# Differential attention over cached keys: scores in pairs of sequences, values in three pieces

## The chip, the core and the metric

One kernel on one NeuronCore of a Trainium2 chip. The metric is the device time of one execution in microseconds (us). TensorE multiplies, VectorE (DVE), ScalarE (ACT) and GpSimd (POOL) do the rest, SyncE (SP) issues most of the transfers. Each engine works through its own list of instructions in order and waits where an operand, a buffer or a transfer isn't ready.

## The reference, cut to the part that matters

The kernel is one layer of a decoder for a prompt of 512 rows and eight sample sequences of 4 new rows each. The part at issue is the differential attention of the samples: each sequence scores its 4 new rows against 256 cached keys (two pages, found through a page table) and its own 4 new keys, in four heads of two 64-wide components; the two softmaxes are subtracted with a factor, and the result is multiplied with the cached and new values.

```
def diff_attend(q, k, v, mask, lam):
    s = jnp.einsum('bqhcd,bkhcd->bhcqk', q, k) * (DA_QK_DIM ** -0.5)
    s = jnp.where(mask[None, None, None], s, -jnp.inf)
    p = jax.nn.softmax(s, axis=-1)
    a = p[:, :, 0] - lam * p[:, :, 1]
    return jnp.einsum('bhqk,bkhd->bqhd', a, v)

def da_attend_sample(q, k, v, lam, past_k, past_v):
    kk = jnp.concatenate([past_k, k], axis=1)
    vv = jnp.concatenate([past_v, v], axis=1)
    return diff_attend(q, kk, vv, kpos[None, :] <= qpos[:, None], lam)
```

## The kernel before

The layer runs in stages: memory keys, mixer input projections, the mLSTM heads, the differential attention with the output projection behind it, cross-attention, and the gated MLP with its convolution. All is fp32 data; large products are made from split weights (a rounded part and a remainder, `split`, lines 144 to 147), so each weight slot passes over ScalarE (cast, L146) and VectorE (remainder, L147) after its transfer.

The differential attention runs two pipelines side by side. The prompt's pipeline (`prompt`, 16 units, one for each of four blocks of rows and four heads; unit i has block i // 4) makes for each unit two score tiles (`da_soft`: product L1211, causal mask L1212, maximum L1214, exponential L1215, combination of the two softmaxes L1217 to L1219), two steps later a turn of the probabilities (`da_turn`, `tpa`, L1227, copied by ScalarE at L1229), one step later the product with the values (`da_av`, `oda`, L1237), and after each block's last head the normed block (`da_post`, `dat`, L1081). The samples' pipeline has eight sequences: the gathers of two key pages (`dk_load`, through `gather`, L1069), their turn into a key tile (`dk_turn`, `tpk`, L1191, copied by ScalarE or VectorE at L1192), and the scores (`dk_scores`, `ssc`, L1197: four heads, each a 32-column instruction into its own 32 partitions, then mask L1199, maximum L1035, exponential L1036). Then follow the softmax of all sequences (`sample_softmax`) and the values (`dv_load`, `dv_out`, `ops`, L1279), again four heads of 32 columns each, for two pages of each sequence; the new keys' values come last (L1287). Both pipelines share five PSUM buffers (`mmp`) for `ssc`, `sda`, `tpa` and `oda`, and three (`at`) for the turns of keys and others.

The gathers of keys and values and the weights' transfers go through one pool of six staging buffers (`stage`, `wst`), in the order of the program: eight key tiles, eight value tiles, then the slots of `w_out`. A tile takes over the buffer of the one six places ahead, and SyncE's list holds these transfers in that order. The turned keys lie in the pool of weight slots (`wp`, four buffers); `W.nslots` limits how many weight slots are fetched ahead. `w_out` is added to the plan only after the samples' values (L1300), and its first product is `proj` (L407 to L409).

The order within each engine's list is set by a scheduler from the order of the program and from priorities; `burst(t)` puts what it holds right behind the instruction t.

Of the kernel before, what the change touches and what calls it, by code (L numbers as in the profile page):

```python
# [15 lines left out]
P = 128  # L16
DM = 1024
SEQ = 512
NB = 8
TS = 4  # L20
NS = NB * TS
ROWS = SEQ + NS
H = 4
# [54 lines left out]
def kernel(ctx: ExitStack, tc: tile.TileContext, I, O):  # L78
    nc = tc.nc
    MUL, ADD, SUB, MAX, MIN = ALU.mult, ALU.add, ALU.subtract, ALU.max, ALU.min  # L80
# [27 lines left out]
    def T2(shape, name, dt=F32):  # L108
        return t2p.tile(list(shape), dt, name=name, tag="T2")
# [4 lines left out]
    def at(name="at"):  # L114
        return psa.tile([P, 512], F32, name=name, tag="at")

    def mmp(name="mm"):
        return psm.tile([P, 512], F32, name=name, tag="mm")
# [8 lines left out]
    def v2(t, b):  # L127
        return t.rearrange("p (a b) -> p a b", b=b)

    mm = nc.tensor.matmul  # L130
    tr = nc.tensor.transpose
    VTT = nc.vector.tensor_tensor
# [22 lines left out]
    def con(n, p=P):  # L155
        o, w = CONST_COLS[n]
        return cpk[:p, o:o + w]
# [49 lines left out]
    W = Weights(NSLOT)  # L207
# [132 lines left out]
    @contextmanager  # L340
    def burst(ins):

        if ins is None:
            yield
        else:
            with tc.issue_after(ins), tc.high_priority():
                yield
# [252 lines left out]
    dvS, kNs = ta[:NS, 0, :], ta[:NS, 1, :]  # L600
# [53 lines left out]
    for c0, c1 in HALF:  # L654
        n = c1 - c0
        ps = mmp()
# [3 lines left out]
        t = T2([64, n], "gt")  # L660
# [38 lines left out]
        in1=v2(Mx[:, 0:SEQ - P], P)[:, :, P - 1:P].broadcast_to([H, 3, P]), op=ADD)  # L699
# [8 lines left out]
    ps = at("gtp")  # L708
# [3 lines left out]
    ps = at("gtp")  # L712
# [190 lines left out]
    ps = at("npt")  # L903
# [7 lines left out]
    for g in range(2):  # L911
        for h in range(0, H, 2):
            t = stage().rearrange("p (j b e) -> p j b e", j=2, b=4)
# [27 lines left out]
    ps = at("nT0")  # L941
# [10 lines left out]
    t = None  # L952
    for h in range(H):
        with burst(t):
            t = mm(pg[NS * h:NS * h + NS, P:2 * P + 1], lhsT=sm_t[:, h, :], rhs=vNs[:, h, :], start=True, stop=True).ins
    for h in range(H):
        with burst(t):
            t = mm(pg[NS * h:NS * h + NS, 4:12], lhsT=qT[:, h, SEQ:], rhs=nT[:, h, :], start=True, stop=True).ins
    for b in range(NB):
        for h in range(H):  # L960
            with burst(t):
                t = mm(pi[NS * h:NS * h + NS, 0:P], lhsT=qzm[:, 256 * h + b * NS:256 * h + (b + 1) * NS],
                       rhs=csts[b // 4, h][:, b % 4, :], start=(b == 0), stop=(b == NB - 1)).ins
# [12 lines left out]
    ps = at("nTt")  # L976
# [17 lines left out]
    r, ss = gq[:, 14:15], gq[:, 15:16]  # L994
# [39 lines left out]
    def sample_exp(sall, b, ps, nm, su):  # L1034
        VRED(out=nm[:, b:b + 1], in_=ps, axis=AX.X, op=MAX, negate=True)  # L1035
        ACT(out=sall[:, b, :], in_=ps, func=AF.Exp, bias=nm[:, b:b + 1], accum_out=su[:, b:b + 1])  # L1036
# [126 lines left out]
    qz = sm.tile([P, H, 2, 2, 16], F32, name="qz", tag="qz", bufs=1)  # L1163
# [8 lines left out]
    for b in range(4):  # L1172
        c = slice(b * P, b * P + P)
# [3 lines left out]
    kst, kts, pts, aTs, outs, rcs = {}, {}, {}, {}, {}, {}  # L1177
# [14 lines left out]
            (VCP if g else nc.scalar.copy)(out=kt[:, :, g * P:(g + 1) * P], in_=v2(ps, P))  # L1192

    def dk_scores(b):
        ps = mmp("ssc")[:, :260]
        for h in range(H):
            mm(ps[NS * h:NS * h + NS], lhsT=qz[:, h, b // 4].rearrange("p c r -> p (c r)"), rhs=kts[b][:, h, :],  # L1197
               start=True, stop=True)
        VTT(out=ps[:, 256:260], in0=ps[:, 256:260], in1=con("cm4"), op=ADD)  # L1199
        sample_exp(sall, b, ps, nm, su)  # L1200

    def da_soft(i):
        b, h = i // H, i % H
# [41 lines left out]
    cv = cst.tile([P, 1], F32, name="cv")  # L1245
    STT(out=cv, in0=con("cB"), scalar=nlam, in1=con("cA"), op0=MUL, op1=ADD)

    W.nslots = 2
    prompt = pipe(4 * H, da_soft, lambda i: None, da_turn, da_av, da_end)
    sall = S([P, NB, 260], F32, "das")  # L1250
    nm, su = small(NB, "snm"), small(NB, "ssu")
    for t, _ in enumerate(pipe(NB, dk_load, dk_turn, dk_scores)):
# [5 lines left out]
    aw, az = sample_softmax(sall, su, cv, con("selD"), "da")  # L1258
# [3 lines left out]
        in1=con("selB").unsqueeze(2).broadcast_to([P, NB, TS]), op=MUL)  # L1262
    nps = at("npn")
    tr(nps[:NS, :P], pz, ident)
    anew = sm.tile([NS, H, NB, TS], F32, name="anew", tag="anew", bufs=1)
    VCP(out=anew, in_=nps[:NS, :P].rearrange("p (b h t) -> p h b t", b=NB, h=H))

    ops = at("ops")
    vts = {}

    def dv_load(b):
        st = vts[b] = stage()
        for g in range(2):
            gather("cache_dv", b, g, st[:, 512 * g:512 * g + 512])

    def dv_out(b):
        for g in range(2):
            for h in range(H):
                mm(ops[NS * h:NS * h + NS, :P], lhsT=az[g][:, h, b * NS:(b + 1) * NS],  # L1279
                   rhs=vts[b][:, g * 512 + h * P:g * 512 + (h + 1) * P], start=(b == 0 and g == 0), stop=False)  # L1280

    for t, _ in enumerate(pipe(NB, dv_load, lambda b: None, dv_out)):
        if t % 2 == 0:
            next(prompt, None)
        F.run(2)
    for h in range(H):
        mm(ops[NS * h:NS * h + NS, :P], lhsT=anew[:, h].rearrange("p b t -> p (b t)"), rhs=dvS[:, h * P:(h + 1) * P],  # L1287
           start=False, stop=True)
    oS = T2([P, P], "daoS")
    nc.scalar.copy(out=oS, in_=ops[:, :P])  # L1290
    sq = T2([P, P], "dasq")
# [2 lines left out]
    ps = at("dat")  # L1294
# [107 lines left out]
    kst, kts, vts = {}, {}, {}  # L1402
# [46 lines left out]
    sall = S([P, NB, 256], F32, "cas")  # L1449
    nm, su = small(NB, "snm"), small(NB, "ssu")  # L1450
# [11 lines left out]
    for b in range(4):  # L1462
        t = mk_scores(b)
    with tc.issue_after(t):
        for j in range(8, 16):
            t = mk_turn(j)
# [7 lines left out]
    with tc.issue_after(t):  # L1474
        for b in range(4, NB):
            t = mk_scores(b)
# [3 lines left out]
    with tc.high_priority():  # L1480
        _, az = sample_softmax(sall, su, None, con("selX"), "ca")
# [15 lines left out]
    ps = at("ost")  # L1497
    for e in range(2):
        tr(ps[:, e * P:(e + 1) * P], oS[:, e * P:(e + 1) * P], ident)
    ps = ps[:, :256].rearrange("p (e h n) -> p h e n", e=2, n=NS)  # L1500
# [20 lines left out]
    for t0 in (0, 4):  # L1521
        ps = at("cvp")
# [5 lines left out]
    ps = at("cvp")  # L1528
# [145 lines left out]
    for gi, js in enumerate(groups):  # L1674
# [47 lines left out]
        if not last:  # L1722
            behind = []
            for n0 in (0, 512):
# [3 lines left out]
                ps = [mmp() for _ in range(4)]  # L1728
                for i in range(nk):
# [3 lines left out]
                    for b in range(4):  # L1733
                        t = one(b, ps[b], i, s)
# [5 lines left out]
            ps = {n0: at("sdn") for n0 in (0, 512)}  # L1740
# [57 lines left out]
        t = chunk(TORD[1], 0)  # L1798

        for n0 in (0, 512):  # L1800
            with burst(t.ins):
                t = chunk(TORD[0], n0)
# [77 lines left out]
```

## Time and profile before

| | us |
|---|---|
| median of 3 runs | 958.01 (953.81 to 958.31) |
| the profiled execution's own time | 956.79 |
| its span in the profile | 955.0 |
| TensorE busy in the span | 932.7 (98%) |
| VectorE busy | 599.2 (63%) |
| ScalarE busy | 388.8 (41%) |
| GpSimd busy | 197.5 (21%) |

The differential attention lies between 246 and 331 us of the span. A busy share is a mean over the stages; how near TensorE is to its limit in one stage is read from its busy time in that stretch, and who holds it up from the waits named beside its rows. Rows of the timeline give start, duration, engine, line, operation and operands; a duration of TensorE reaches into the next instruction, so costs are taken from start to start.

### The profile page before, as it was taken

What the parts mean: (1) busy time and instruction counts of PE and PEld (TensorE: products, weight loads), DVE (VectorE), ACT (ScalarE), POOL (GpSimd) and SP (SyncE); (2) the same over time, 40 slices, a digit from 0 to 9 for tenths busy, and PEclk for the clock granted to TensorE, in tenths of its full rate; (3) what the DMA queues carried; (4) which work ended last, traced back from release to release, by engine and by line L of the source; (5) the groups of instructions that cost most, each with busy time, mean ns of one, the idle gap of its engine ahead of it and who ended that gap; (6) DMA issues with size and microseconds to landing.
All of it is one profiled execution on the core that took longest, in us unless ns stands there. A gap on an engine that the chain in (4) does not pass through costs nothing. (4 is left out here: it accounts for less than half of the span.)

```text
span 955.0 us, 17088 instructions
## 1 busy us (share of the span) xinstructions
PE 932.7 (98%) x6619; PEld 810.6 (85%) x6619; DVE 599.2 (63%) x1129; ACT 388.8 (41%) x750; POOL 197.5 (21%) x383
## 2 busy tenths in 40 slices
PE   8999999999999999999999999999999999999995
PEld 5899777879866778998777799989988997999974
DVE  5745144565887448635654769727758676676867
ACT  5655133344676447624544523332212222222232
POOL 6610000024432217300000444001110110111114
PEclk9999999999999999999999999999999999999998
DMA  8950023334825429955953743063053302512023
GB/s 278 309 184 2 1 89 136 89 110 150 264 90 183 155 94 329 307 155 167 353 213 114 206 134 89 4 177 89 4 144 79 122 26 79 165 48 89 24 92 116
DMA packets 120674, 130.27 MB, mean 136 GB/s; under 512 B 8568, under 2 KB 86233, under 8 KB 120593
## 3 DMA queue, kind: packets, MB, share of 16 engines
q1 hardware_dynamic: 114408, 125.69, 41.9%
q10 hardware_dynamic: 6184, 3.48, 1.2%
q8 instruction: 52, 0.85, 0.4%
q14 instruction: 30, 0.24, 0.1%
HBM read 112.22 MB, written 16.93 MB: 135 GB/s over the span
## 5 line engine op out<-in xcount | busy, mean ns | idle before, releaser
L146 ACT CAST wslot<-wst 128x1024 fp32r<-128x1024 f32 x125 | 130.9, 1050 | 259.9 <-issue 74.7
L477 PE MATMUL mm<-fT,wslot 128*128 128x256 f32 x1872 | 235.9, 288 | 0.0
L477 PEld LDWEIGHTS mm<-fT,wslot 128*128 128x128 f32 x1872 | 234.4, 188 | 1.8 <-issue 0.8
L147 DVE TENSOR_TENSOR wslot<-wst,wslot 128x1024 fp32r<-128x1024 f32 x125 | 155.1, 1245 | 89.3 <-ACT wslot L146 88.8
L1691 PE MATMUL mm<-wslot,act 128*128 128x512 f32 (+1 forms) x180 | 70.2, 391 | 0.0
L1692 PE MATMUL mm<-wslot,act 128*128 128x512 f32 (+1 forms) x180 | 70.0, 392 | 0.0
L1690 PE MATMUL mm<-wslot,act 128*128 128x512 f32 (+1 forms) x180 | 69.3, 387 | 0.0
L1598 POOL COPY cvo<-u 128x2 f32<-128x2 f32 x43 | 11.0, 256 | 204.8 <-DVE u L1596 194.7
L407 PE MATMUL mm<-wslot,hT 128*128 128x512 f32 x128 | 52.2, 408 | 0.0
L409 PE MATMUL mm<-wslot,hT 128*128 128x512 f32 x128 | 51.5, 403 | 0.0
L408 PE MATMUL mm<-wslot,hT 128*128 128x512 f32 x128 | 51.3, 401 | 0.0
L477 PE MATMUL mm<-hT,wslot 128*128 128x256 f32 (+1 forms) x384 | 51.0, 289 | 0.0
L1593 DVE TENSOR_TENSOR u<-mm,rsb 128x256 f32<-128x256 f32 x43 | 18.2, 424 | 51.0 <-PE mm L477 50.1
L477 PEld LDWEIGHTS mm<-hT,wslot 128*128 128x128 f32 x384 | 49.2, 188 | 0.5 <-issue 0.2
L1690 PEld LDWEIGHTS mm<-wslot,act 128*128 128x128 f32 x180 | 34.3, 191 | 8.0 <-issue 0.8
L1691 PEld LDWEIGHTS mm<-wslot,act 128*128 128x128 f32 x180 | 33.8, 188 | 7.2
L1692 PEld LDWEIGHTS mm<-wslot,act 128*128 128x128 f32 x180 | 33.8, 188 | 7.2 <-issue 0.4
L1610 ACT ACTIVATE c<-c 128x560 f32<-128x560 f32 x21 | 14.1, 672 | 56.7 <-DVE c L1604 56.7
L1604 DVE SCALAR_TENSOR_TENSOR c<-u,cvT,c 128x560 f32<-128x560 f32 x43 | 34.3, 798 | 0.9
L1603 DVE SCALAR_TENSOR_TENSOR c<-u,cvT,c 128x560 f32<-128x560 f32 x43 | 34.1, 793 | 0.2
L1703 DVE TENSOR_TENSOR yp<-mm,yp 128x512 f32<-128x512 f32 (+1 forms) x41 | 27.2, 674 | 5.1 <-PE mm L1692 5.0
L409 PEld LDWEIGHTS mm<-wslot,hT 128*128 128x128 f32 x128 | 24.5, 191 | 5.3
(474 smaller groups left out, 1857.7 us busy)
## 6 DMA issues: line engine op xcount, KB each, us to landing
wst<-in_w_up_dram SPq DMA_DIRECT2D x42, 512.0 KB
wst<-in_w_in_dram SPq DMA_DIRECT2D x28, 512.0 KB
wst<-in_w_down_dram SPq DMA_DIRECT2D x20, 512.0 KB
wst<-in_cache_mem_k_dram SPq DMA_DIRECT2D x16, 512.0 KB
wst<-in_w_mk_dram SPq DMA_DIRECT2D x8, 512.0 KB
xb<-in_x_prompt_dram SPq DMA_DIRECT2D x8, 512.0 KB
wst<-in_cache_dk_dram SPq DMA_DIRECT2D x16, 256.0 KB
wst<-in_cache_dv_dram SPq DMA_DIRECT2D x16, 256.0 KB
```

The costliest lines, as they stand in the source:

```text
L146: nc.scalar.copy(out=hi, in_=src)
L147: (eng or nc.vector).tensor_tensor(out=lo, in0=src, in1=f32(hi), op=SUB)
L407: mm(ps[b], lhsT=xt.hi(k, c0, c0 + n), rhs=s[:, 0, kk, :], start=(k == 0), stop=False)
L408: mm(ps[b], lhsT=xt.hi(k, c0, c0 + n), rhs=s[:, 1, kk, :], start=False, stop=False)
L409: return mm(ps[b], lhsT=xt.lo(k, c0, c0 + n), rhs=s[:, 0, kk, :], start=False, stop=(k == nk - 1))
L477: mm(ps[i], lhsT=s[:, l, k, :], rhs=x(k, c0, c1), start=(k == 0 and j == 0), stop=(k == 7 and j == 2))
L1603: STT(out=c, in0=u[:, 1:EXT - 1], scalar=w[1], in1=c, op0=MUL, op1=ADD)
L1604: STT(out=c, in0=u[:, 0:EXT - 2], scalar=w[0], in1=c, op0=MUL, op1=ADD)
L1690: mm(ps, lhsT=t[:, 0, c0:c0 + P], rhs=s[:, 0, i % 2, cs], start=st, stop=False)
L1691: mm(ps, lhsT=t[:, 0, c0:c0 + P], rhs=s[:, 1, i % 2, cs], start=False, stop=False)
L1692: return mm(ps, lhsT=t[:, 1, c0:c0 + P], rhs=s[:, 0, i % 2, cs], start=False, stop=en)
L1703: VTT(out=y, in0=ps, in1=y, op=ADD)
```

## The change

Scores: `dk_scores` does nothing at even sequences, and at odd ones the products of the sequence and of the one ahead of it, eight instructions in one unbroken piece; the masks, maxima and exponentials of both follow. Values: `dv_out` does nothing except at sequences 2, 5 and 7, where it does 24, 24 and 16 products in one piece each, later sequences first, and at the last the new keys' four products right behind. `W.nslots` is 0 during the scoring and 2 again afterwards.

```
     def dk_scores(b):
-        ps = mmp("ssc")[:, :260]
-        for h in range(H):
-            mm(ps[NS * h:NS * h + NS], lhsT=qz[:, h, b // 4]..., rhs=kts[b][:, h, :], start=True, stop=True)
-        VTT(out=ps[:, 256:260], in0=ps[:, 256:260], in1=con("cm4"), op=ADD)
-        sample_exp(sall, b, ps, nm, su)
+        if b % 2 == 0:
+            return
+        pair = {}
+        t = None
+        for c in (b, b - 1):
+            pair[c] = mmp("ssc")[:, :260]
+            for h in range(H):
+                with burst(t):
+                    t = mm(pair[c][NS * h:NS * h + NS], lhsT=qz[:, h, c // 4]..., rhs=kts[c][:, h, :],
+                           start=True, stop=True).ins
+        for c, ps in pair.items():
+            VTT(out=ps[:, 256:260], in0=ps[:, 256:260], in1=con("cm4"), op=ADD)
+            sample_exp(sall, c, ps, nm, su)
...
-    W.nslots = 2
+    W.nslots = 0
     prompt = pipe(4 * H, da_soft, lambda i: None, da_turn, da_av, da_end)
...
+    W.nslots = 2
+    DV = {2: [(2, 1), (2, 0), (1, 0), (1, 1), (0, 0), (0, 1)], 5: [(5, 1), (5, 0), (4, 0), (4, 1), (3, 0), (3, 1)],
+          7: [(7, 1), (7, 0), (6, 0), (6, 1)]}
     def dv_out(b):
-        for g in range(2):
+        t = None
+        for c, g in DV.get(b, []):
             for h in range(H):
-                mm(ops[NS * h:NS * h + NS, :P], lhsT=az[g][:, h, b * NS:(b + 1) * NS], ...)
+                with burst(t):
+                    t = mm(ops[NS * h:NS * h + NS, :P], lhsT=az[g][:, h, c * NS:(c + 1) * NS], ...).ins
+        if b == NB - 1:
+            for h in range(H):
+                with burst(t):
+                    t = mm(ops[NS * h:NS * h + NS, :P], lhsT=anew[:, h]..., rhs=dvS[:, h * P:(h + 1) * P],
+                           start=False, stop=True).ins
...
-    for h in range(H):
-        mm(ops[NS * h:NS * h + NS, :P], lhsT=anew[:, h]..., rhs=dvS[:, h * P:(h + 1) * P], start=False, stop=True)
```

The change moves instructions; SyncE's list stays the same row for row. First place: TensorE around the scores of sequences 2 and 3 (`ssc`), before. `x4` counts instructions in a row.

```order
L1197 MATMUL ssc<-kT,qz 32x260 x4
L1191 MATMUL tpk<-cpk,wst 128x128 x4
L1237 MATMUL oda<-dvN,aT 128x128
L1191 MATMUL tpk<-cpk,wst 128x128 x8
L1227 MATMUL tpa<-cpk,pda 128x128
L1211 MATMUL sda<-dkT,dqT 128x256
L1212 LDWEIGHTS cb
L1212 MATMUL sda<-cb 128x128
```

And in the change, from a little later on:

```order
L1245 MATMUL oda<-dvN,aT 128x128
L1191 MATMUL tpk<-cpk,wst 128x128 x4
L1235 MATMUL tpa<-cpk,pda 128x128
L1219 MATMUL sda<-dkT,dqT 128x256
L1220 LDWEIGHTS cb
L1220 MATMUL sda<-cb 128x128
L1191 MATMUL tpk<-cpk,wst 128x128 x8
L1219 MATMUL sda<-dkT,dqz 128x256
L1220 LDWEIGHTS cb
L1220 MATMUL sda<-cb 128x128
L1204 MATMUL ssc<-kT,qz 32x260 x8
```

The piece of sequence 2, which stood ahead of the turn of the third unit (`tpa`), now stands behind it, joined to sequence 3's.

Second place: VectorE from the combination of unit 12's softmaxes (`pda`, 128x512) to that of unit 13's, before. `wslot` are the remainders of `w_out`'s slots, `nm` the maxima of the prompt's scores.

```order
L1219 SCALAR_TENSOR_TENSOR pda<-pda,rc 128x512
L147 TENSOR_TENSOR wslot<-wst,wslot 128x1024
L1214 TENSOR_REDUCE nm<-sda 128x1 x2
L147 TENSOR_TENSOR wslot<-wst,wslot 128x1024 x2
L1217 RECIPROCAL rc<-su 128x2
L1214 TENSOR_REDUCE nm<-sda 128x1
L1218 TENSOR_SCALAR rc<-rc,su,nlam 128x1
L1219 SCALAR_TENSOR_TENSOR pda<-pda,rc 128x512
L147 TENSOR_TENSOR wslot<-wst,wslot 128x1024
```

And in the change:

```order
L1227 SCALAR_TENSOR_TENSOR pda<-pda,rc 128x512
L147 TENSOR_TENSOR wslot<-wst,wslot 128x1024
L1222 TENSOR_REDUCE nm<-sda 128x1
L147 TENSOR_TENSOR wslot<-wst,wslot 128x1024
L1222 TENSOR_REDUCE nm<-sda 128x1
L147 TENSOR_TENSOR wslot<-wst,wslot 128x1024 x2
L1225 RECIPROCAL rc<-su 128x2
L1222 TENSOR_REDUCE nm<-sda 128x1
L1226 TENSOR_SCALAR rc<-rc,su,nlam 128x1
L1222 TENSOR_REDUCE nm<-sda 128x1
L1227 SCALAR_TENSOR_TENSOR pda<-pda,rc 128x512
```

The fourth remainder and the second maximum of unit 14, which stood behind unit 13's combination (the last maximum just outside the rows of before), now stand ahead of it.

Third place: ScalarE over the same time, before. `wslot` are the casts of `w_out`'s slots, `dao` the evacuated value products, `aT` the turned probabilities, `daoS` the samples' values.

```order
L1215 ACTIVATE pda,su<-sda,nm 128x512 x2
L146 CAST wslot<-wst 128x1024
L1239 ACTIVATE dao<-oda,rc 128x128
L1229 COPY aT<-tpa 128x384
L146 CAST wslot<-wst 128x1024 x2
L1215 ACTIVATE pda,su<-sda,nm 128x512 x2
L1239 ACTIVATE dao<-oda,rc 128x128
L1229 COPY aT<-tpa 128x512
L146 CAST wslot<-wst 128x1024
L1215 ACTIVATE pda,su<-sda,nm 128x512
L1290 COPY daoS<-ops 128x128
```

And in the change:

```order
L1223 ACTIVATE pda,su<-sda,nm 128x512 x2
L146 CAST wslot<-wst 128x1024
L1247 ACTIVATE dao<-oda,rc 128x128
L1237 COPY aT<-tpa 128x384
L146 CAST wslot<-wst 128x1024 x2
L1223 ACTIVATE pda,su<-sda,nm 128x512
L146 CAST wslot<-wst 128x1024
L1308 COPY daoS<-ops 128x128
L1223 ACTIVATE pda,su<-sda,nm 128x512
L1247 ACTIVATE dao<-oda,rc 128x128
L1237 COPY aT<-tpa 128x512
```

The fourth cast and the copy of the samples' values stand now between unit 13's two exponentials, ahead of the copy `aT` of unit 12 that follows them.

## Rows read from the trace of the kernel before

**Rows 1.** The page: busy time and TensorE's busy tenths in 40 slices.

```profile
PE 932.7 (98%) x6619; PEld 810.6 (85%) x6619; DVE 599.2 (63%) x1129; ACT 388.8 (41%) x750; POOL 197.5 (21%) x383
...
PE   8999999999999999999999999999999999999995
```

**Rows 2.** Windows: length, busy PE, PEld, DVE, ACT, POOL; granted clock, DMA share, GB/s.

```profile
96.00:99.50 3.50, 3.50 (x16) 2.38 (x16) 0.28 (x2) 0.00 (x0) 0.00 (x0) 0.51 0.00 0
246.00:285.00 39.00, 36.55 (x299) 26.32 (x299) 33.17 (x103) 31.32 (x107) 15.09 (x19) 1.00 0.56 183
285.00:305.00 20.00, 19.93 (x213) 12.59 (x212) 14.69 (x27) 14.16 (x33) 2.10 (x4) 1.00 0.64 218
```

**Rows 3.** Timeline, TensorE: start, duration, instruction, [idle before, releaser]; three waits.

```profile
260.58 0.30 PE L1227 MATMUL tpa<-cpk,pda 128*128 128x128 f32 x1 [0.74 <-DVE pda L1219]
...
270.18 0.41 PE L1227 MATMUL tpa<-cpk,pda 128*128 128x128 f32 x2 [0.62 <-ACT pda L1215]
...
282.73 0.44 PE L1060 MATMUL spt<-cpk,spc 128*128 128x128 f32 x2 [0.70 <-ACT spc L1057]
```

**Rows 4.** Timeline, VectorE, 295 to 302 us.

```profile
295.17 1.23 DVE L147 TENSOR_TENSOR wslot<-wst,wslot 128x1024 fp32r<-128x1024 f32 x1 [1.06 <-ACT wslot L146]
296.32 1.28 DVE L1214 TENSOR_REDUCE nm<-sda 128x1 f32<-128x512 f32 x2
297.52 2.35 DVE L147 TENSOR_TENSOR wslot<-wst,wslot 128x1024 fp32r<-128x1024 f32 x2
...
300.91 0.75 DVE L1219 SCALAR_TENSOR_TENSOR pda<-pda,rc 128x512 f32<-128x512 f32 x1
```

**Rows 5.** Timeline, TensorE, 301 to 305 us.

```profile
301.72 0.65 PE L1227 MATMUL tpa<-cpk,pda 128*128 128x128 f32 x4
...
304.23 0.47 PE L407 MATMUL mm<-wslot,mixT 128*128 128x512 f32 x1
```

**Rows 6.** Timeline, TensorE: around a score piece.

```profile
264.94 0.22 PE L1212 MATMUL sda<-cb 128*128 128x128 bf16 x1
265.00 0.61 PE L1191 MATMUL tpk<-cpk,wst 128*128 128x128 f32 x4
...
265.88 0.22 PE L1212 MATMUL sda<-cb 128*128 128x128 bf16 x1
266.02 0.65 PE L1197 MATMUL ssc<-kT,qz 128*32 128x260 f32 x8
```

**Rows 7.** Timeline, TensorE: value pieces and what follows; xN counts passes, two an instruction.

```profile
288.12 0.94 PE L1237 MATMUL oda<-dvN,aT 128*128 128x128 f32 x6
...
291.20 1.08 PE L1279 MATMUL ops<-wst,daz 128*32 128x128 f32 x32
292.21 0.94 PE L1237 MATMUL oda<-dvN,aT 128*128 128x128 f32 x6
...
298.52 0.65 PE L1279 MATMUL ops<-wst,daz 128*32 128x128 f32 x16
299.10 0.42 PE L1287 MATMUL ops<-ta,anew 32*32 32x128 f32 x8
```

**Rows 8.** Timeline, SyncE: issues of sequence 6's values, and of w_out.

```profile
286.54 0.85 SPq L1069 DMA_DIRECT2D wst<-in_cache_dv_dram  x2
...
288.74 10.85 SPq L231 DMA_DIRECT2D wst<-in_w_out_dram  x6
```

**Rows 9.** Timeline, ScalarE: first cast, copy of unit 12, fourth cast of w_out.

```profile
294.10 1.04 ACT L146 CAST wslot<-wst 128x1024 fp32r<-128x1024 f32 x1 [1.28 <-DMA wst<-in_w_out_dram]
...
300.05 0.59 ACT L1229 COPY aT<-tpa 128x512 f32<-128x512 f32 x1
300.52 1.07 ACT L146 CAST wslot<-wst 128x1024 fp32r<-128x1024 f32 x1
```

**Rows 10.** Timeline, VectorE and ScalarE: maximum and exponential of one sequence's scores.

```profile
272.54 0.43 DVE L1035 TENSOR_REDUCE snm<-ssc 128x1 f32<-128x260 f32 x1
...
273.06 0.48 ACT L1036 ACTIVATE das<-ssc,snm 128x260 f32<-128x260 f32 x1 [0.38 <-DVE rc L1217]
```

More of the change, by code (lines that the diff above doesn't have):

```diff
@@ L1194, in dk_scores @@
     def dk_scores(b):
-        ps = mmp("ssc")[:, :260]
-        for h in range(H):
-            mm(ps[NS * h:NS * h + NS], lhsT=qz[:, h, b // 4].rearrange("p c r -> p (c r)"), rhs=kts[b][:, h, :],
-               start=True, stop=True)
-        VTT(out=ps[:, 256:260], in0=ps[:, 256:260], in1=con("cm4"), op=ADD)
-        sample_exp(sall, b, ps, nm, su)
+        if b % 2 == 0:
[6 more added lines that the diff above has]
+                with burst(t):
+                    t = mm(pair[c][NS * h:NS * h + NS], lhsT=qz[:, h, c // 4].rearrange("p c r -> p (c r)"), rhs=kts[c][:, h, :],
+                           start=True, stop=True).ins
+        for c, ps in pair.items():
+            VTT(out=ps[:, 256:260], in0=ps[:, 256:260], in1=con("cm4"), op=ADD)
+            sample_exp(sall, c, ps, nm, su)
     def da_soft(i):
@@ L1274, in dv_load @@
             gather("cache_dv", b, g, st[:, 512 * g:512 * g + 512])
+    W.nslots = 2
+    DV = {2: [(2, 1), (2, 0), (1, 0), (1, 1), (0, 0), (0, 1)], 5: [(5, 1), (5, 0), (4, 0), (4, 1), (3, 0), (3, 1)],
+          7: [(7, 1), (7, 0), (6, 0), (6, 1)]}
     def dv_out(b):
-        for g in range(2):
+        t = None
+        for c, g in DV.get(b, []):
             for h in range(H):
-                mm(ops[NS * h:NS * h + NS, :P], lhsT=az[g][:, h, b * NS:(b + 1) * NS],
-                   rhs=vts[b][:, g * 512 + h * P:g * 512 + (h + 1) * P], start=(b == 0 and g == 0), stop=False)
+                with burst(t):
+                    t = mm(ops[NS * h:NS * h + NS, :P], lhsT=az[g][:, h, c * NS:(c + 1) * NS],
+                           rhs=vts[c][:, g * 512 + h * P:g * 512 + (h + 1) * P], start=((c, g) == DV[2][0]), stop=False).ins
+        if b == NB - 1:
+            for h in range(H):
+                with burst(t):
+                    t = mm(ops[NS * h:NS * h + NS, :P], lhsT=anew[:, h].rearrange("p b t -> p (b t)"), rhs=dvS[:, h * P:(h + 1) * P],
+                           start=False, stop=True).ins
     for t, _ in enumerate(pipe(NB, dv_load, lambda b: None, dv_out)):
@@ L1285 @@
         F.run(2)
-    for h in range(H):
-        mm(ops[NS * h:NS * h + NS, :P], lhsT=anew[:, h].rearrange("p b t -> p (b t)"), rhs=dvS[:, h * P:(h + 1) * P],
-           start=False, stop=True)
     oS = T2([P, P], "daoS")
```

## The prediction

> **What bounds the kernel now.** I read the busy shares first, then TensorE's busy time by stretches, then the rows of the stretch that the change touches, one engine after the other. TensorE is busy 98% of the span [rows 1]. From 285 to 305 us it is busy 19.93 of 20 us and from 246 to 285 us 36.55 of 39 [rows 2]: 2.45 us of idle time lie in the scoring stretch, and next to none behind it. So a microsecond less of TensorE work is a microsecond less of time only where no other engine is just behind TensorE. Here others are: three named waits of TensorE, 0.74, 0.62 and 0.70 us, end with VectorE or ScalarE work [rows 3], and at 301.72 TensorE starts the turn of a head's probabilities when VectorE's last step on them, 300.91 plus 0.75, has just ended at 301.66 [rows 4, 5]. That coincidence decides the case.
>
> Notation: unit i is one of the prompt's 16 (12 to 15 are the 512-column ones); v0 to v7 are the gathered value tiles of the eight sequences; w0 to w3 are the first four slots of w_out.
>
> **The change, part by part.**
>
> *Fewer pieces.* TensorE pays at each end of a run of 32-column instructions. Into it: a full-width instruction follows a mask product after 0.06 us (264.94 to 265.00), a score piece after 0.14 (265.88 to 266.02) [rows 6], so 0.08. Out of it: 32 value passes take 1.01 us (291.20 to 292.21), 16 take 0.58 (298.52 to 299.10) [rows 7]; 16 more cost 0.43, so 0.15 is fixed. Together 0.23 us. Score pieces go from 8 to 4, value pieces from 5 to 3 (the first is split by a turn now). Six fewer: 6 x 0.23 = 1.4 us of TensorE time. The passes themselves stay.
>
> *Key tiles in the weight slots.* The slot limit goes from 2 to 0 during scoring. By then the plan of weights is used up (w_out is added after it), and SyncE's order is the same row for row. I cost it at nothing, and nothing hides it: there is nothing to issue.
>
> *Scoring order.* The first score piece of a pair now stands where the second stood. Sequence 2's piece stood ahead of the 0.74 us wait at 260.58 and stands behind it now; the wait ends with VectorE, which does the same work up to there, so the piece's 0.65 us [rows 6] is lost again. Ahead of the wait at 270.18, VectorE had one mask addition; now two additions and two maxima stand there, and they need the whole pair: about 0.5 us later. The wait at 282.73 is for ScalarE's copy, behind two exponentials before and behind one now: some 0.5 us earlier. Four merges give 4 x 0.23 = 0.9. Sum: -0.9 + 0.65 + 0.5 - 0.5 = -0.25 us at 285 us. Bounds: 3.4 us earlier if all 2.45 of idle time went too, 4 us later if the pairs' own chain is uncovered (second rival). I take -0.25, nearest to the rows.
>
> *The value pieces and SyncE.* The stage pool has six buffers; v6 takes over v0's, v7 v1's, w0 v2's. Now v0 is released in the middle of the first stretch of value work, and v6 is issued at 286.54, w0 at 288.74 [rows 8]. In the change the first piece holds v2, v1, v0 in that order, so v0 comes free with the piece's last pass. The value work up to v2 ended at 288.12 with a turn in its middle [rows 7]; less 0.25 and one edge of 0.23 that is 287.6, so v6 is issued near 287.7. Two issues take 0.85 from the first start to the second end [rows 8], about 0.52 from start to start; four issues stand ahead of w0 on SyncE, v6's two and v7's two: 287.7 + 2.1 = 289.8, or 1.05 us later than now. The transfers are as many, so w0 lands 1.05 us later: its cast on ScalarE, released by the DMA at 294.10 [rows 9], starts near 295.15. v3 to v5 all come free with the second piece, so w1 to w3 are not late; w3 even comes early, which is what moves the orders of ScalarE and VectorE.
>
> *ScalarE and VectorE behind it.* Both work in order. VectorE now does: split w0 (295.17), two maxima, splits w1 and w2 (297.52), a maximum, the combination of unit 13 (300.91 to 301.66), then split w3 and another maximum [rows 4]. From 295.17 to 301.66 these add up to nearly all of the time: it is a chain. In the change split w3 and both maxima of unit 14 stand ahead of the combination: a split is 1.15 (2.35 for two, with the overlap), a maximum 0.6 (1.28 for two) [rows 4], together 1.75. The combination ends at 301.66 + 1.05 + 1.75 = 304.45. On ScalarE the copy of unit 12's turned probabilities (300.05) stands ahead of cast w3 (300.52, 1.07 long) now and behind it in the change [rows 9], with the copy of the value sums too: 300.05 + 1.05 + 1.0 + 0.25 = 302.35. TensorE waits for that before the value product of unit 12 and then for VectorE before the turn of unit 13: 304.5 instead of 301.72, 2.8 us later [rows 5]. The last scores follow, then the projection, which starts at 304.23 now while one small turn moves from ahead of it to behind its start: 2.7 us later [rows 5]. The gain of 1.4 is inside this figure: it became waiting time.
>
> *From there on* TensorE shows nine tenths or more in every slice but the last [rows 1], and weights come as it frees slots, so nearly all of it stays. If a late transfer absorbs some, at most about 1 us.
>
> **Sum.** The profiled execution's own time is 956.79 us, 955.0 of it span; 956.79 + 2.7 = 959.5. The three runs' median, 958.01, lies 1.2 higher; against it the forecast is 1.5 up. Either way it is within 0.5% (4.8 us), about what a measurement of this kernel can tell from no change.
>
> **Rivals.**
> 1. *Only the edges count.* If w0 lands as early as now, or VectorE and ScalarE keep ahead, the 1.4 us stay saved: 955.4. For it: busy TensorE, no idle time from 285 to 305. Against it: the 0.06 us between the combination and the turn [rows 4, 5].
> 2. *The pairs starve TensorE (slower than before).* Five PSUM buffers serve the score, turn, value and output tiles of a step; before, a step took five, now every other step takes six. So the second score tile of a prompt head must wait until the pair's first tile has been added to, reduced and exponentiated: a maximum of 0.43 and an exponential of 0.48, with the small addition ahead some 1.1 us of VectorE and ScalarE work [rows 10]. Uncovered in all four pairs it costs 4.4 us: 959.5 + 4.4 = 963.9, slower by 0.7%. It decides where less than 1.1 us of TensorE work stands between a pair and those scores; at the first pair some 2 us of turns stand there, so I expect it covered mostly.
> 3. *The clock.* The new waits are near 2 us long. What rows show: the one stretch near half speed amid the work, 96.0 to 99.5 us at a granted 0.51 (1.2 of 2.4 GHz), has TensorE busy throughout, and 2.45 us of gaps from 246 us kept 1.00 [rows 2]. If each of two waits set off a stretch like it, 2 x 3.5 x 0.49 = 3.4 us more: 962.9.
> The Trainium skill, "TensorE: Matmul & The Clock Gate", section "HAM oscillation", says that gaps in TensorE's work bring it back to half rate, so that what follows starts cold. By that rule this rival would be the likelier one; the trace does not bear it out, since its one drop amid the work has no gap in it.
> 4. *The change doesn't do what it says.* The order shows the four pairs and three pieces unbroken, so this holds only for the weight slots, and there it costs nothing.
>
> **How the numbers follow.** Forecast 0.55, only the edges 0.28, starved pairs 0.12, clock 0.05. The predicted time is 959.5. The range 955.0 to 962.5 holds the forecast with 2 us for its terms and executions (the runs shown differ by 4.5), and the first rival; it leaves out most of rivals 2 and 3 and a small tail below. Slower by over 0.5%: 0.13, most of rivals 2 and 3. Faster by over 0.5% would need all idle time of the scoring stretch and the edges: 0.04. The rest, 0.83, is no change to be told.
>
> **What would show it.** Right: four score and three value pieces; w_out's first cast starting 1 us later in relation to the first value piece; ScalarE's cast w3 ahead of the copy for unit 12; a TensorE wait of 1 to 2.5 us before unit 13's turn and one before unit 12's value product, named VectorE and ScalarE; the projection starting near 307. Wrong: the projection starting at 303, with no wait from 295 to 305 (rival 1); waits for ScalarE's exponentials ahead of prompt scores before 281 (rival 2); a granted clock under 1.00 after 300 (rival 3).

## The result, and the profile after

| | before | after |
|---|---|---|
| median, 22 runs each | 958.36 us (953.81 to 961.80) | 960.37 us (959.13 to 963.22) |
| ratio to before, 95% interval | | 1.0023 (1.0012 to 1.0034) |
| the profiled execution's own time | 956.79 | 961.08 |
| its span | 955.0 | 959.3 |

The changed kernel is slower by 2.2 us in 958. That lies within the 0.5% that the prediction calls no change, and it was forecast at 959.5. It can be told from no change only because there are 22 runs of each. A second set of 12 runs gave 1.0019 (1.0001 to 1.0037).

The page of the kernel after, to be read against [rows 1]: TensorE's busy time is the same to 0.4 us, its share is 97% in place of 98%, and one slice, the thirteenth (288 to 312 us), is not full any more.

```profile
PE 932.3 (97%) x6619; PEld 810.8 (85%) x6619; DVE 601.9 (63%) x1129; ACT 388.5 (40%) x750; POOL 197.3 (21%) x383
...
PE   8999999999998999999999999999999999999995
```

Windows of after, columns as in [rows 2]:

```profile
285.00:305.00 20.00, 16.35 (x188) 10.68 (x177) 13.48 (x24) 12.79 (x29) 2.42 (x3) 0.96 0.66 218
...
297.00:300.00 3.00, 1.31 (x5) 0.39 (x3) 3.00 (x4) 2.88 (x6) 0.00 (x0) 1.00 0.98 345
300.00:303.00 3.00, 1.24 (x10) 0.97 (x8) 3.00 (x6) 2.92 (x9) 0.74 (x2) 1.00 0.27 79
303.00:306.00 3.00, 2.80 (x8) 1.59 (x9) 1.52 (x5) 0.88 (x3) 0.00 (x0) 0.56 0.00 0
```

From 285 to 305 us, where TensorE had 0.07 us of idle time [rows 2], it now has 3.65. Nearly all of it lies between 297 and 303 us, and there VectorE is busy all the time. TensorE is held up by engines that are themselves full. Behind that, from 303 to 306, the granted clock is 0.56.

Executions differ by a microsecond or two ahead of the stage (the half-speed stretch at 96 us in [rows 2] is missing in this one), so all kernels are compared over one **stretch**: from the first causal-mask product of unit 0 (`sda<-cb`) to the projection's first product. TensorE's timeline of before has its start at 247.90 and the samples' first value piece (`ops`) at 285.76:

```profile
247.90 0.22 PE L1212 MATMUL sda<-cb 128*128 128x128 bf16 x1
...
285.76 0.85 PE L1279 MATMUL ops<-wst,daz 128*32 128x128 f32 x22
```

With 304.23 from [rows 5] the stretch of before is 56.33 us. TensorE's timeline of after:

```profile
245.89 0.22 PE L1220 MATMUL sda<-cb 128*128 128x128 bf16 x1
...
283.97 0.60 PE L1081 MATMUL dat<-cpk,dasq 128*128 128x128 f32 x4
284.51 1.52 PE L1295 MATMUL ops<-wst,daz 128*32 128x128 f32 x48
...
298.90 1.13 PE L1219 MATMUL sda<-dkT,dqz 128*128 128x512 f32 x2 [1.69 <-ACT pda L1223]
...
301.42 1.16 PE L1245 MATMUL oda<-dvN,aT 128*128 128x128 f32 x8 [1.33 <-ACT aT L1237]
...
303.20 0.98 PE L1235 MATMUL tpa<-cpk,pda 128*128 128x128 f32 x4 [0.62 <-DVE pda L1227]
...
307.23 0.47 PE L407 MATMUL mm<-wslot,mixT 128*128 128x512 f32 x1
```

The stretch of after is 307.23 - 245.89 = 61.34 us, 5.01 more. Three waits, 1.69 + 1.33 + 0.62 = 3.64 us, stand where before had none: unit 14's second score waits for unit 13's exponential (which, read with the pool of five PSUM buffers, frees the buffer that it needs), unit 12's value product for ScalarE's copy, unit 13's turn for VectorE's combination. From that turn to the projection it is 4.03 us, against 2.51 before [rows 5]: the half clock.

What stands ahead of the releasers is read on their engines, first ScalarE after (to be read against [rows 9]):

```profile
295.79 1.05 ACT L146 CAST wslot<-wst 128x1024 fp32r<-128x1024 f32 x1 [1.15 <-DMA wst<-in_w_out_dram]
297.12 1.04 ACT L146 CAST wslot<-wst 128x1024 fp32r<-128x1024 f32 x1 [0.29 <-DMA wst<-in_w_out_dram]
298.08 0.68 ACT L1223 ACTIVATE pda<-sda,nm 128x512 f32<-128x512 f32 x1
...
298.75 1.03 ACT L146 CAST wslot<-wst 128x1024 fp32r<-128x1024 f32 x1
299.69 0.26 ACT L1308 COPY daoS<-ops 128x128 f32<-128x128 f32 x1
...
300.76 0.60 ACT L1237 COPY aT<-tpa 128x512 f32<-128x512 f32 x1
```

and VectorE after (to be read against [rows 4]):

```profile
298.61 2.43 DVE L147 TENSOR_TENSOR wslot<-wst,wslot 128x1024 fp32r<-128x1024 f32 x2
...
302.40 0.74 DVE L1227 SCALAR_TENSOR_TENSOR pda<-pda,rc 128x512 f32<-128x512 f32 x1
```

Unit 13's first exponential (298.08) stands behind the casts of w1 and w2, which wait for their transfers; unit 12's copy (300.76) stands behind the cast of w3 and the samples' copy; the combination (302.40) stands behind the remainders of w2 and w3 and behind both maxima of unit 14.

### The profile page after: what moved, and what is told of

Read it like the earlier page. It is cut to its first block, busy times and chain, and to the rows that moved or that the text cites. A ratio compares the mean times of both kernels' runs of the same rounds, so it can differ in the third digit from the quotient of the medians.

```text
span 959.3 us, 17085 instructions
## 1 busy us (share of the span) xinstructions
PE 932.3 (97%) x6619; PEld 810.8 (85%) x6619; DVE 601.9 (63%) x1129; ACT 388.5 (40%) x750; POOL 197.3 (21%) x383
```

## The experiments

All ratios are to the kernel before on the same chip, with 95% intervals. Unit and slot numbers are those of the prediction. The table puts the runs together; "waits" are TensorE's named waits from 295 us to the projection, in us, and "clock" names stretches at half speed between 20 and 940 us.

| kernel | ratio | stretch, us | waits | clock |
|---|---|---|---|---|
| before | | 56.33 | none | 96 |
| after | 1.0023 (1.0012 to 1.0034) | 61.34 | 1.69, 1.33, 0.62 | 303 |
| after_again | 1.0019 (1.0001 to 1.0037) | 58.74 | 0.77, 1.34, 0.62 | 96 |
| values_only | 1.0023 (1.0012 to 1.0034) | 58.43 | 0.52, 1.33, 0.84 | 96, 551 |
| pairs_only | 0.9999 (0.9986 to 1.0013) | 56.63 | 0.38 | 96, 483, 551 |
| v0_first | one run | 59.22 | 1.25, 1.33, 0.62 | none |
| held_w3 | 1.0005 (0.9988 to 1.0021) | 57.23 | 0.45, 0.88 | 96 |
| held_w123 | 1.0012 (0.9999 to 1.0024) | 57.71 | 2.13 | 96 |
| held_late2 | 0.9980 (0.9963 to 0.9996) | 55.60 | none | 96 |
| late2_again | 0.9994 (0.9978 to 1.0009) | 56.02 | 0.18 | none |
| late_half | 0.9987 (0.9970 to 1.0005) | 56.81 | none | none |
| late_single | 0.9982 (0.9968 to 0.9995) | 55.50 | none | 546 |

### One half of the change each: values_only and pairs_only

values_only has before's scores and after's value pieces:

```
 def dk_scores(b):
-    if b % 2 == 0: return
-    for c in (b, b - 1): ...
+    ps = mmp("ssc")[:, :260]
+    for h in range(H): mm(ps[NS * h:NS * h + NS], ...)
```

> Before's scores (one sequence a piece), the changed kernel's value pieces. Read on the stretch from unit 0's first mask product (sda<-cb, 247.90 before, 245.89 after) to the projection's first product (304.23 before, 307.23 after): 56.33 us before, 61.34 after. Theory (w_out's casts and splits, brought late by the value pieces, stand ahead of unit 13's softmax): the TensorE waits in front of unit 12's value product and unit 13's turn stay, 3 us or more between 295 and 305, and the stretch is 60 to 62 us if the clock falls behind them as it did after the change, 58.5 to 59.5 if it does not; ratio to before 1.001 to 1.004. Rival, the paired scores are the cause (they put the first value piece 0.2 to 0.8 us later): the waits fall under 1 us together and the stretch is at most 57.0; ratio 0.998 to 1.000. Rival, only edges count: stretch 56.0, ratio 0.9995.

TensorE's timeline of values_only:

```profile
247.56 0.22 PE L1212 MATMUL sda<-cb 128*128 128x128 bf16 x1
...
299.13 1.12 PE L1211 MATMUL sda<-dkT,dqz 128*128 128x512 f32 x2 [0.52 <-ACT pda L1215]
...
301.64 1.16 PE L1237 MATMUL oda<-dvN,aT 128*128 128x128 f32 x8 [1.33 <-ACT aT L1229]
...
303.64 0.66 PE L1227 MATMUL tpa<-cpk,pda 128*128 128x128 f32 x4 [0.84 <-DVE pda L1219]
...
305.99 0.48 PE L407 MATMUL mm<-wslot,mixT 128*128 128x512 f32 x1
```

The three waits are there without the pairs, 2.69 us together (3 or more were expected), the clock is 1.00 behind them, and the stretch is 58.43, a little under the 58.5 to 59.5 expected for that case. The ratio is that of the whole change; that it agrees to the fourth digit is chance, with intervals of 0.0011 either side. The value pieces are the cause, and the fall of the clock in after's profile is not needed to explain the time.

pairs_only is the other half: after's scores, and before's `dv_out` with one piece a sequence and the new keys' products behind the loop. `W.nslots` is 0 during its scoring too, and is not set back to 2 for the values.

```
 def dv_out(b):
-    for c, g in DV.get(b, []): ...
+    for g in range(2): ...
```

> The changed kernel's paired scores, before's value pieces (one a sequence). Theory: the two waits of the scoring stage after the change (0.3 and 1.1 us for unit 4's and unit 5's combinations) are here too, the four value pieces saved by the change are not, and no wait over 0.5 us is new behind the first value piece compared with before; stretch 56.0 to 57.0 against 56.33, ratio 0.999 to 1.001, granted clock 1.00 up to the projection. Rival, the pairs are the cause: the stretch is 58.5 us or more, with waits of 3 us between 295 and 305.

The stretch is 304.01 - 247.38 = 56.63 us, the ratio 0.9999, and one wait is new behind the first value piece, 0.38 us for unit 13's combination. So the pairs cost 0.30 us here instead of gaining 0.92 from four saved pieces. Where that goes stands in the scoring stretch; TensorE's timeline of pairs_only, waits only:

```profile
259.59 0.33 PE L1235 MATMUL tpa<-cpk,pda 128*128 128x128 f32 x1 [0.31 <-DVE pda L1227]
269.94 0.41 PE L1235 MATMUL tpa<-cpk,pda 128*128 128x128 f32 x2 [1.06 <-DVE pda L1227]
281.96 0.44 PE L1060 MATMUL spt<-cpk,spc 128*128 128x128 f32 x2 [0.49 <-ACT spc L1057]
282.90 0.94 PE L1245 MATMUL oda<-dvN,aT 128*128 128x128 f32 x6 [0.40 <-ACT aT L1237]
```

With two more at 250.73 and 251.92, 0.31 and 0.54 for the key tiles' copies, they are 3.11 us; the four of before (0.74, 0.62 and 0.70 in [rows 3] and one of 0.32) are 2.38. The saved 0.92 less 0.73 of waits leaves 0.19 us; the wait of 0.38 turns that into a loss of 0.19, and the other 0.11 was not followed. All of it is within what was expected.

The profiles repeat this price up to the first value piece. From unit 0's first mask product to that piece it is 38.61 or 38.62 us in all seven profiles with four pairs and the three value pieces, and 38.30 and 38.29 in the two with single scores and the same value pieces (values_only and late_single, below). With before's value pieces it is 38.18 in pairs_only against 37.86. So the pairs cost 0.32 us there, whatever stands behind them.

### Holding w_out's work back: held_w3 and held_w123

If the waits come from where w_out's casts and remainders stand, moving those alone must move the waits. `held_w3` is after, with w3's cast behind unit 12's copy on ScalarE and its remainder behind unit 13's combination on VectorE:

```
+        if share == 'held' and h:
+            with tc.issue_after(marks[h[0]]):
+                nc.scalar.copy(out=sv[:, 0], in_=st)
+            with tc.issue_after(marks[h[1]]):
+                VTT(out=sv[:, 1], in0=st, in1=f32(sv[:, 0]), op=SUB)
...
+    HOLD[0] = [None, None, None, (('turn', 12), ('comb', 13))]
```

> The changed kernel with one order more: the cast of w3 (the fourth 512-column slot of w_out) stands on ScalarE behind the copy of unit 12's turn, and its split on VectorE behind unit 13's combination. Theory: what is late at unit 13's turn is VectorE's split of w3 (1.2 us) and at unit 12's value product ScalarE's cast of w3 (1.0 us) and its landing; each of these waits gets shorter by 0.6 to 1.3 us, the wait for unit 13's softmax in front of its second score (1.7 us, behind the casts of w1 and w2) stays, and the projection begins 1.5 to 2.5 us sooner: stretch 59 to 60 us if the clock still falls, 57 to 58 if it does not; ratio to before 1.000 to 1.001. Rival, the waits go with the value tiles' and not with w_out's order: all three stay within 0.3 us, stretch 61, ratio 1.002.

What this calls unit 13's second score is unit 14's. The wait for the combination went altogether, the one at unit 12's value product fell from 1.33 to 0.88 us, less than expected, and the first was 0.45; the stretch is 57.23. TensorE's timeline of held_w3:

```profile
298.35 1.13 PE L1230 MATMUL sda<-dkT,dqz 128*128 128x512 f32 x2 [0.45 <-ACT pda L1234]
...
300.41 1.16 PE L1256 MATMUL oda<-dvN,aT 128*128 128x128 f32 x8 [0.88 <-ACT aT L1248]
```

`held_w123` holds w1 and w2 too, their casts behind unit 13's exponentials:

```
-    HOLD[0] = [None, None, None, (('turn', 12), ('comb', 13))]
+    HOLD[0] = [None, (('exp', 13), ('comb', 13)), (('exp', 13), ('comb', 13)), (('turn', 12), ('comb', 13))]
```

> The changed kernel with w1, w2 and w3 held back: their casts on ScalarE behind unit 13's exponentials (w3's behind unit 12's copy), their splits on VectorE behind unit 13's combination. Theory: all three waits of 295 to 304 (1.7, 1.3 and 0.6 us) go, TensorE stays busy, the clock does not fall before the projection, and the stretch is 54.5 to 56.5 us, under before's 56.33 by what the fewer pieces save (0.9 to 1.4 us) unless w1 to w3 are now late for the projection's own products, which would show as waits of 1 to 2 us behind 302; ratio to before 0.998 to 1.000. Rival, the slots are not what is late: the waits stay, ratio 1.002.

Half of this missed: the waits for the exponential and the combination went, but that for the copy grew to 2.13 us, and the stretch was 57.71. ScalarE's timeline of held_w123 shows why, with the product that waited behind it on TensorE's:

```profile
298.02 1.99 ACT L223 CAST wslot<-wst 128x1024 fp32r<-128x1024 f32 x2
...
300.32 0.60 ACT L1248 COPY aT<-tpa 128x512 f32<-128x512 f32 x1
```

```profile
300.97 1.16 PE L1256 MATMUL oda<-dvN,aT 128*128 128x128 f32 x8 [2.13 <-ACT aT L1248]
```

L223 is the held cast. Two casts of 1.99 us now stood between unit 13's exponentials and unit 12's copy. The miss says the same as the theory: whichever of the prompt's steps stands behind these casts is the one that TensorE waits for.

### The clock: after_again

The changed kernel once more, unedited.

> The changed kernel once more, for the clock and for the size of the waits. In its first profile TensorE's clock fell to 0.56 of full speed from 303 to 306 us, behind 3.6 us of waits, and no half-speed stretch stood at 96 to 99 us, where before and four other profiles have one. Theory A (the stretch at half speed is one that every execution has somewhere, and the waits do not decide whether it is there): the waits of 295 to 304 are 2.5 to 3.7 us again, and the clock is 1.00 from 300 to 310 with a drop at 96 us, or falls at 303 with no drop at 96; in the first case the stretch from unit 0's first mask product to the projection is 58.4 to 59.8 us (values_only: 58.43). Theory B (the waits set it off): clock under 0.7 near 303 again, with or without the drop at 96, stretch 61 to 61.5. Ratio to before 1.001 to 1.0035 by both.

TensorE's timeline, and a window (columns as above):

```profile
247.95 0.22 PE L1220 MATMUL sda<-cb 128*128 128x128 bf16 x1
...
300.04 1.13 PE L1219 MATMUL sda<-dkT,dqz 128*128 128x512 f32 x2 [0.77 <-ACT pda L1223]
...
302.56 1.16 PE L1245 MATMUL oda<-dvN,aT 128*128 128x128 f32 x8 [1.34 <-ACT aT L1237]
...
304.34 0.66 PE L1235 MATMUL tpa<-cpk,pda 128*128 128x128 f32 x4 [0.62 <-DVE pda L1227]
...
306.69 0.47 PE L407 MATMUL mm<-wslot,mixT 128*128 128x512 f32 x1
```

```profile
303.00:309.00 6.00, 5.38 (x27) 3.66 (x26) 4.52 (x12) 4.11 (x10) 0.63 (x2) 1.00 0.06 22
```

2.73 us of waits, the clock at 1.00 behind them, the drop back at 96 us, a stretch of 58.74: the first case of theory A. From the turn to the projection it is 2.35 us here against 4.03 in after's profile, so the half clock cost that execution 1.68 us, and its longer first wait (1.69 against 0.77, behind w1's transfer) 0.92; together they are the 2.60 between the two stretches. But the other half of theory A, that every execution has such a drop somewhere, fell with v0_first, late_half and late2_again, which have none.

### The order of the value tiles: v0_first

```
-    DV = {2: [(2, 1), (2, 0), (1, 0), (1, 1), (0, 0), (0, 1)], 5: ..., 7: ...}
+    DV = {2: [(0, 0), (0, 1), (1, 0), (1, 1), (2, 0), (2, 1)], 5: ..., 7: ...}
```

> The changed kernel with the tiles of each value piece in ascending order (v0, v1, v2; v3, v4, v5; v6, v7). The prediction's step (v6 takes v0's buffer, and v0 is the last of the first piece): v6's first issue comes some 0.9 us earlier in relation to the first value piece (now 0.70 behind its start), w_out's first issue and first cast likewise 0.9 us earlier, and the waits of 295 to 304 shrink by about 1 us. Reading of the trace after (v6 takes the buffer that comes free first, whichever tile lay in it): first issue 0.6 to 0.8 us behind the piece's start as now, w_out's first issue 2.7 to 2.8 behind it, waits within 0.5 us of those of values_only or of the changed kernel, stretch 58.4 to 61.4 us.

SyncE's timeline of v0_first, under TensorE's first value piece:

```profile
283.41 1.52 PE L1295 MATMUL ops<-wst,daz 128*32 128x128 f32 x48
```

```profile
284.19 1.94 SPq L1069 DMA_DIRECT2D wst<-in_cache_dv_dram  x4
286.24 7.81 SPq L231 DMA_DIRECT2D wst<-in_w_out_dram  x6
```

v6's first issue comes 0.78 us behind the piece's start and w_out's 2.83, in after 0.70 and 2.75:

```profile
285.21 1.94 SPq L1069 DMA_DIRECT2D wst<-in_cache_dv_dram  x4
287.26 7.89 SPq L231 DMA_DIRECT2D wst<-in_w_out_dram  x6
```

The order within a piece makes no difference here. By these times v6 is issued about when the piece's first tile is through (16 passes take 0.58 us, [rows 7]), whichever that is; the rows don't name the buffer. That contradicts the rule, stated ahead of the prediction and used in it, that a tile takes over the buffer of the one six places ahead. The waits are 3.20 us together and the stretch 59.22, within what the second reading expected.

### Nothing of w1 to w3 ahead of units 12 and 13: held_late2, late2_again

```
-    HOLD[0] = [None, (('exp', 13), ('comb', 13)), (('exp', 13), ('comb', 13)), (('turn', 12), ('comb', 13))]
+    HOLD[0] = [None, (('turn', 12), ('comb', 13)), (('exp', 14, 0), ('comb', 13)), (('exp', 14, 1), ('comb', 13))]
...
+    with tc.issue_after(marks['turn', 12]):
+        nc.scalar.copy(out=oS, in_=ops[:, :P])
```

> The changed kernel with w1, w2, w3 and the samples' value copy all behind unit 12's turn copy on ScalarE (w2's cast behind unit 14's first exponential, w3's behind its second), their splits on VectorE behind unit 13's combination. In held_w123 the casts of w1 and w2 stood ahead of unit 12's copy and cost 2.13 us; here nothing of w_out but w0 stands ahead of units 12 and 13. Theory: no wait of more than 0.3 us between 285 and the projection, which begins 302.3 to 303.0 us after a first mask product at 246.55, a stretch of 55.7 to 56.4 (before 56.33); w1 to w3 are needed 1.4, 2.8 and 4.2 us into the projection and are there, or cost under 1 us; ratio 0.9985 to 1.0000. Rival: the waits move on into the projection as they moved in held_w123, stretch as said but 1 to 2 us of waits from 303 to 310; ratio 1.000 to 1.001.

> held_late2 once more beside late_single, on the same chip: no wait over 0.3 us between 285 and the projection, stretch from unit 0's first mask product to the projection 55.4 to 55.8 us (55.60 in its first profile, 56.33 before), ratio to before 0.998 to 0.9995. If the ratio of 0.998 was a lucky one, it lies near 0.9995, which the stretch alone gives (0.73 us of 957).

TensorE is busy 20.00 of 20 us where after had 16.35; unit 12's copy comes close behind unit 13's exponentials, and the cast of w1 behind it. A window of held_late2 and ScalarE's timeline:

```profile
285.00:305.00 20.00, 20.00 (x216) 13.39 (x216) 13.80 (x25) 13.72 (x33) 3.17 (x3) 1.00 0.66 218
```

```profile
298.94 0.59 ACT L1248 COPY aT<-tpa 128x512 f32<-128x512 f32 x1
...
299.56 1.08 ACT L223 CAST wslot<-wst 128x1024 fp32r<-128x1024 f32 x1
```

The stretches are 55.60 and 56.02 us, the second above its 55.4 to 55.8; no wait moved into the projection. The ratios are 0.9980 and 0.9994. The 0.42 us between the two profiles of one kernel go with w0: its cast starts 8.31 and 8.73 us behind the first value piece, and the projection 16.99 and 17.40. The next two kernels fit (8.51 and 17.18 in late_half, 8.53 and 17.21 in late_single). So w0, still ahead of unit 13's maxima on VectorE, is what the projection's start goes by now; holding it back too was not tried, and stretches of single profiles scatter by 0.4 us with it. The same three value pieces that cost 2.1 to 2.4 us are paid back by an order of ScalarE's and VectorE's lists. That ties the loss to that order.

### Fewer or no pairs on top: late_half and late_single

`late_half` pairs only sequences 2, 3 and 6, 7; `late_single` has before's scores.

> held_late2 with only sequences 2, 3 and 6, 7 scored as pairs, 0, 1, 4 and 5 singly. The pairs of the change save 0.23 us each, and the waits of the scoring stretch grew from 2.38 us in four (before) to 3.17 us in six (pairs_only). Theory: the wait of 0.54 behind the first pair and the growth from 0.62 to 1.06 behind the third go, the wait of 0.74 comes back in part; from the first mask product to the samples' first turn (spt, 34.83 us before, 34.58 with all pairs) 34.2 to 34.6 us, ratio 0.1 per mille either side of held_late2. Rival, a pair only moves a wait that VectorE and ScalarE set anyway: 34.6 to 34.9.

Both expectations missed: from the first mask product to the samples' first turn it is 282.68 - 247.09 = 35.59 us, against 34.83 before and 34.58 with all pairs. One wait is longer (1.18 us at 259.69, for ScalarE's exponential) and one new (0.88 at 275.47, ahead of a pair, released by VectorE). This mixed order is the longest of the three, in one profile; which instruction of the other engines sets that was not followed further.

> held_late2 with before's scores, one sequence a piece. By the parts measured so far: the pairs alone made the stretch 0.30 us longer (pairs_only 56.63 against 56.33), so without them 55.3 us, and no wait from 285 to the projection; ratio 0.0003 under that of late2_again, which is less than the interval can tell. Rival, the pairs pay once nothing behind them waits: 55.9 us or more (their four pieces of 0.23 us come back).

300.59 - 245.09 = 55.50 us, no wait behind 285 us, ratio 0.9982 (0.9968 to 0.9995). The forecast of 55.3 is 0.2 off, and the rival (55.9 or more) is out: the pairs don't pay even when nothing waits behind them, by the 0.32 us measured up to the first value piece. late_single has the shortest stretch. It is faster than after: the intervals of the ratios don't meet, and ratio over ratio it is about 0.4%. Against before its interval lies just under 1, but so did held_late2's in its first set, and not in its second; so a small gain is likely and its size not settled. The stretch explains 0.83 us; the 1.7 us that the ratio stands for are not told apart from that. From held_late2 it can't be told apart by time either.

## Why the prediction was right, step by step

The forecast was 959.5 and the median came out at 960.37; as a ratio to its own base the forecast was 1.0028, the measurement 1.0023 and 1.0019. From w0's cast on the mechanism is the one forecast: casts and remainders of `w_out` ahead of the steps that TensorE waits for. How w0 came to be late is not, and its part of the agreement is luck, as told below. After_again starts the stage within 0.05 us of before (247.95 and 247.90), so its times can be put beside the forecast's directly:

| step of the prediction | forecast | after_again |
|---|---|---|
| samples' first turn, against 282.73 before (scoring order, -0.25) | 282.48 | 282.54 |
| w0's cast | 295.15 | 295.23 |
| copy of unit 12's turn | 302.35 | 301.91 |
| turn of unit 13 | 304.5 | 304.34 |
| projection | near 307 | 306.69 |

SyncE's and ScalarE's rows of after_again for this table and for what follows (w_out's issues, w0's cast, unit 12's copy):

```profile
289.33 7.89 SPq L231 DMA_DIRECT2D wst<-in_w_out_dram  x6
```

```profile
295.23 1.04 ACT L146 CAST wslot<-wst 128x1024 fp32r<-128x1024 f32 x1 [2.51 <-DMA wst<-in_w_out_dram]
...
301.91 0.60 ACT L1237 COPY aT<-tpa 128x512 f32<-128x512 f32 x1
```

*Fewer pieces.* Borne out where it can be read: in after's timeline a pair takes 1.02 us from its start to the next instruction's (260.21 to 261.23, below), and in before a single score piece takes 0.58, from 266.02 [rows 6] to 266.60; twice that less one pair is 0.14, and the 0.08 ahead of a piece is saved as well.

```profile
260.21 1.08 PE L1204 MATMUL ssc<-kT,qz 128*32 128x260 f32 x16
261.23 1.09 PE L1191 MATMUL tpk<-cpk,wst 128*128 128x128 f32 x8
```

And TensorE's timeline of before, behind the single piece:

```profile
266.60 0.49 PE L1237 MATMUL oda<-dvN,aT 128*128 128x128 f32 x2
```

All six come to 1.4 us by these edges. Against before, after_again's named waits over the stretch are 3.46 us longer and the stretch is 2.41, so 1.05 us of the saving show there, and more than all of it was lost in waits, as forecast.

*Weight slots.* Costed at nothing. It was not undone alone on the chip. pairs_only has the limit of 0 too and took 0.9999 of before's time, so that it costs something by itself is not seen.

*Scoring order.* The -0.25 us is right at the samples' first turn, but not all of its parts are. The wait of 0.62 became 1.05 and that of 0.70 became 0.50 (forecast 0.5 more and 0.5 less; the first is near, the second measured 0.2); that of 0.74, in which the prediction lost sequence 2's piece again (at 0.65 us, the row's duration; from start to start a piece takes 0.58), became 0.31, and a new one of 0.53 came behind the first pair (252.49) in its place. And the step stops short. In after_again the second exponential of a prompt unit, which stood ahead of the samples' copy on ScalarE, stands behind it and ahead of the copy `aT`, and a wait of 0.40 us for that copy is new (283.48). ScalarE's timeline of after_again:

```profile
282.11 0.38 ACT L1057 COPY spc<-spa 128x260 f32<-128x260 f32 x1 [0.55 <-PE spa L1055]
282.38 0.59 ACT L1223 ACTIVATE pda<-sda,nm 128x384 f32<-128x384 f32 x1
...
282.95 0.48 ACT L1237 COPY aT<-tpa 128x384 f32<-128x384 f32 x1
```

*Value pieces and SyncE.* The size is right and the way to it wrong, so that 295.15 met 295.23 is luck. The prediction had v6 take over v0's buffer at the piece's end, and so SyncE 1.05 us late. By the times of v0_first v6 goes out behind the first tile of the piece, and in relation to the piece w_out's first issue is no later than before (2.75 us behind its start; before 288.74 - 285.76 = 2.98). What is late is the piece: 286.57 in after_again against 285.76, since the turn `dat` of a finished block (0.54 us in after's timeline) moved ahead of it and the scoring lost 0.2 (0.2 gained at the samples' first turn, 0.4 lost for the copy behind it). Of the 1.13 us that w0's cast came later, 0.59 stand at w_out's first issue (289.33 against 288.74), where the prediction put 1.05; the other 0.54 lie between that issue and the cast (5.90 us against 5.36), which the prediction took as unchanged. So w0's cast came 1.1 us later in the span but only 0.3 in relation to the first value piece, where the prediction's list of signs wanted 1 us.

*ScalarE and VectorE behind it.* Right in order and releasers, and near in time: TensorE waits for ScalarE before unit 12's value product (1.34 us) and for VectorE before unit 13's turn (0.62, where the list of signs wanted 1 to 2.5). The combination ended at 303.54 + 0.74 = 304.28 in after_again; the prediction's sum for it, 301.66 + 1.05 + 1.75, is 304.46 and not 304.45, which changes nothing. Not seen was a third, for unit 13's exponential behind the casts of w1 and w2, 0.5 to 1.7 us. It took a part of what was forecast for the other two; the end of the chain is the same.

*From there on.* Held: the stretch of after_again is 2.4 us longer and the ratio corresponds to 1.8 to 2.2 us.

*Rivals.* Only the edges (955.4): out, since the waits came; it is what held_late2 and late_single show, with stretches 0.3 to 0.8 us under before. Starved pairs: out at that price, the pairs cost 0.3 us where the rival had 4.4. The clock, given 0.05: it did fall in one profile, behind the waits, and cost 1.7 us there, which is what the rival put on each of its two stretches. In after_again, values_only and v0_first, with 2.7 to 3.2 us of the same waits, it did not. The runs without a profile say the same: in the set of after_again the mean granted clock is 0.992 in the 12 runs of the changed kernel and in the 29 of before, so more half-speed time is not what makes it slower. (In the set of values_only it is 0.9925 against 0.9938, so there the clock may have taken a part of the ratio; the 2.1 us by which its stretch is longer are at 1.00.) The 0.05 was the chance that the clock decides the time, and it didn't; the drop itself came in one of four profiles. The Trainium skill, "TensorE: Matmul & The Clock Gate", section "HAM oscillation", says that gaps in TensorE's work bring it back to half rate; after's profile agrees (0.56 behind 3.6 us of gaps), the three others don't (1.00 behind 2.7 to 3.2 us of gaps), so the runs here leave the rule open at gaps of this size.

## What to carry to other kernels

Before a change of pieces on an engine that is busy nearly all the time, look for the place where another engine's chain ends within a tenth of a microsecond of it; if the scheduler moves one more instruction ahead of that chain's end, the gain turns into waiting, and more. Here 1.4 us of saved pieces became 2 us of loss because a weight slot's cast came 1 us later and one more cast and remainder stood ahead of the steps that TensorE needed next. The remedy was to hold back what is not needed yet: w1 to w3 were wanted by the projection only, and placing them behind the due steps took the waits away and brought the time back to before's or a little under it.

## What the runs showed of the hardware that was not expected

The half-speed stretches of TensorE's clock, 3 to 4 us each, come and go between executions of like kernels: at 96 us in seven of the twelve profiles, with TensorE busy throughout, near 483 or 550 in three, at 303 in one, and none at all between 20 and 940 us in three. Ahead of those near 483 and 550 TensorE was busy 3.7 to 4.1 of 5 us; but v0_first, busy 3.70 of 5 us from 545 to 550, kept 1.00 behind them, so such gaps alone don't tell whether a drop comes. The one at 303 cost 1.68 us (4.03 against 2.35 us for the same work), which is nearly the size of the whole effect. A span of a single execution can't decide a change of 0.2%; a stretch between two marks that holds no such drop comes nearer, to the 0.4 us by which two profiles of one kernel differ.

w1 was late for its cast by 1.15 us in one profile of the changed kernel and not at all in the next, with the same issues behind the same piece; what the transfers met in between stays open.
